# RMSNorm and QKV projection: the last two 128-column stores issued from two queues

## Chip, cores, metric

One core of one Trainium2 chip runs the kernel. The metric is the device time in microseconds (us). Executions of one program scatter by some tenths of a microsecond, so each figure is a median with its range.

## The reference

`x` is 8 x 1024 x 768 in float32, `w_qkv` is 768 x 2304, `gamma` has 768 ones.

```python
rms = np.sqrt(np.mean(x ** 2, axis=-1, keepdims=True) + eps)
x_norm = x / rms * gamma
return np.matmul(x_norm, w_qkv).astype(np.float32)
```

## The kernel before

The 8192 rows are 64 row tiles of 128. For each, SP (the sync engine, which here only issues DMAs) loads `x`, VectorE casts it to bf16, a DMA transpose on SP's queue turns it (`xbar`; `xT<-xb` in the profile), PE (the matmul engine) multiplies it with the resident weights in column blocks of 512, VectorE and ScalarE take turns to bring the blocks out of PSUM (times 1/rms; one such step is an eviction), and SP stores them. In the lines of the profile DVE is VectorE, ACT is ScalarE, PEld are PE's weight loads, and SPq and ACTq are the sequencers of SP and ScalarE, which issue DMAs; L255 is line 255 of the kernel. The author sets the order by writing a planned time beside each piece of work; the plan is sorted and emitted, and every engine then runs its own list in order. So a planned time is only a place in a list: nothing waits for it. The cut below leaves out what `...` stands for, and its comments are mine.

```python
    def width(t, n0):
        return P if t == MT - 1 and n0 >= N - 2 * P else min(NT, N - n0)
    ...
    def store(t, h, n0, nl):
        p0 = PARTS[h][0]
        nc.sync.dma_start(out=of[t * P:(t + 1) * P, n0:n0 + nl], in_=OUT[t, h][:, n0 - p0:n0 - p0 + nl])
    ...
    def evac_at(time, t, n0, eng, gap):
        at(time, evac, t, n0, eng)
        ...
        if t >= MT - 2:
            at(time + gap - 0.5, store, t, h, n0, nl)      # the last two row tiles: a store per block
        elif left[t, h] == 0:
            at(time + gap, store, t, h, *PARTS[h])
    ...
    for t in range(HEAD, MT):                              # HEAD = 6
        ahead = 6.0 if t < HEAD + 5 else 0.0
        ...                                                # load at now - 15 - ahead, cast at now - 8.5 - ahead
        at(now - 7.5 - ahead, xbar, t)
        ...
        for n0 in [*range(0, N, NT)] + [N - P] * (t == MT - 1):
            at(now, mm, t, n0, range(KO))
            now += width(t, n0) * US
            flip ^= 1
            evac_at(now + 0.2, t, n0, "DVE" if flip else "ACT", gap=1.2)
```

The very last 256 columns are computed as two blocks of 128, the first brought out by ScalarE, the second by VectorE. `ahead` gives 6 us of extra lead to the row tiles 6 to 10.

Of the kernel before, what the change touches and what calls it, by code (L numbers as in the profile page):

```python
# [92 lines left out]
def kernel(  # L93
# [8 lines left out]
    nc = tc.nc  # L102
# [6 lines left out]
    of = out.flatten_outer_dims()  # L109
    M, K = xf.shape  # L110
    Kw, N = w_qkv.shape
    assert K == Kw
    P = 128
    KO = K // P
    MT = M // P
# [35 lines left out]
    X, XB, XT, RS, OUT, WF, PM, PT = {}, {}, {}, {}, {}, {}, {}, {}  # L151
# [100 lines left out]

    def store(t, h, n0, nl):
        p0 = PARTS[h][0]
        nc.sync.dma_start(out=of[t * P:(t + 1) * P, n0:n0 + nl], in_=OUT[t, h][:, n0 - p0:n0 - p0 + nl])  # L255



# [12 lines left out]
    def evac_at(time, t, n0, eng, gap):  # L271
        at(time, evac, t, n0, eng)
        h = part(n0)
        nl = width(t, n0)
        left[t, h] = left.get((t, h), PARTS[h][1]) - nl
        if t >= MT - 2:
            at(time + gap - 0.5, store, t, h, n0, nl)
        elif left[t, h] == 0:
            at(time + gap, store, t, h, *PARTS[h])
# [79 lines left out]
```

## Time and profile before

| | before |
|---|---|
| median of the 3 executions known at the prediction | 388.34 us (388.09 to 388.74) |
| span of the profiled execution | 386.86 us |
| PE busy | 379.9 us (98%) |
| last 512-column eviction of VectorE begins | 382.56 us |
| from there to the end of the span, the "tail" | 4.30 us |

The profile is of one execution. The span runs from its first to its last instruction and is some 1.8 us shorter than the device time (388.64 us for this execution). The DMA strips show the mean busy share of the 16 DMA engines in 40 slices of a window, in tenths. The lines themselves are in the prediction.

### The profile page before, as it was taken

What the parts mean: (1) busy time and instruction counts of PE and PEld (TensorE: products, weight loads), DVE (VectorE), ACT (ScalarE), POOL (GpSimd) and SP (SyncE); (2) the same over time, 40 slices, a digit from 0 to 9 for tenths busy, and PEclk for the clock granted to TensorE, in tenths of its full rate; (3) what the DMA queues carried; (4) which work ended last, traced back from release to release, by engine and by line L of the source; (5) the groups of instructions that cost most, each with busy time, mean ns of one, the idle gap of its engine ahead of it and who ended that gap; (6) DMA issues with size and microseconds to landing.
All of it is one profiled execution on the core that took longest, in us unless ns stands there. A gap on an engine that the chain in (4) does not pass through costs nothing.

```text
span 386.9 us, 5470 instructions
## 1 busy us (share of the span) xinstructions
PE 379.9 (98%) x1927; PEld 192.2 (50%) x1965; DVE 153.4 (40%) x307; ACT 181.6 (47%) x365; POOL 6.5 (2%) x14
## 2 busy tenths in 40 slices
PE   8999999999999999999999999999999999999996
PEld 4444655454554554554554554554554554554553
DVE  2744534434333344333344333343333343333332
ACT  4752644453544443544444444544444534434532
POOL 0130000000000000000000000000000000000000
PEclk9999999999999999999999999999999999999999
DMA  8999999999999999999999999999999999999985
GB/s 291 390 281 402 398 318 363 344 338 283 351 297 308 303 295 321 293 300 322 305 289 313 285 318 312 293 309 275 326 311 297 304 317 305 304 306 289 292 264 186
DMA packets 89719, 119.91 MB, mean 310 GB/s; under 512 B 52438, under 2 KB 61532, under 8 KB 89692
## 3 DMA queue, kind: packets, MB, share of 16 engines
q1 hardware_dynamic: 89680, 119.56, 101.2%
q8 instruction: 15, 0.25, 0.3%
q14 instruction: 12, 0.10, 0.1%
q10 hardware_dynamic: 12, 0.00, 0.0%
HBM read 32.25 MB, written 75.50 MB: 279 GB/s over the span
## 4 chain that ended last, share of the span: by engine, by line
PE 89%; DMA 8%; issue 1%; DVE 1%; ACT 1%; SPq 0%
PE pm L235 89%; DMA x_t<-in_x_dram 3%; DMA w_f<-in_w_qkv_dram 2%; DMA xT<-xb 2%; DMA out_dram<-ot 1%; ACT ot L251 1%; DVE ot L249 0%; DVE xb L174 0%; SPq L160 0%; SPq L155 0%; SPq L255 0%; ACT w_b L168 0%
## 5 line engine op out<-in xcount | busy, mean ns | idle before, releaser
L235 PE MATMUL pm<-w_b,xT 128*128 128x512 bf16 (+1 forms) x1888 | 372.1, 357 | 2.1
L235 PEld LDWEIGHTS <-xT 128*128 128x128 bf16 x1926 | 187.9, 98 | 185.5 <-DMA xT<-xb 0.5
L249 DVE TENSOR_SCALAR ot<-pm,rstd 128x512 f32<-128x512 f32 (+1 forms) x161 | 111.5, 695 | 206.1 <-PE pm L235 201.7
L251 ACT ACTIVATE ot<-pm,rstd 128x512 f32<-128x512 f32 (+2 forms) x160 | 102.7, 643 | 191.7 <-PE pm L235 151.0
L185 ACT ACTIVATE sq<-x_t 128x768 bf16<-128x768 f32 x64 | 53.4, 834 | 3.0 <-DMA x_t<-in_x_dram 3.0
L174 DVE CAST xb<-x_t 128x768 bf16<-128x768 f32 x61 | 33.2, 545 | 13.6 <-DMA x_t<-in_x_dram 13.5
L187 ACT ACTIVATE rms<-ssq,eps_sb 128x1 f32<-128x1 f32 x64 | 18.8, 294 | 2.1
L185 ACT ACTIVATION_READ_ACCUMULATOR sq<-x_t 128x1 f32 x64 | 12.2, 191 | 0.0
L166 DVE TENSOR_SCALAR w_b<-w_f,g_sb 128x512 bf16<-128x512 f32 (+1 forms) x16 | 7.7, 499 | 5.9 <-DMA w_f<-in_w_qkv_dram 5.9
L192 DVE RECIPROCAL rstd<-rms 128x1 f32<-128x1 f32 x64 | 9.8, 153 | 0.0
L170 POOL TENSOR_SCALAR w_b<-w_f,g_sb 128x512 bf16<-128x512 f32 (+1 forms) x8 | 5.8, 735 | 23.5 <-DMA w_f<-in_w_qkv_dram 23.5
L284 PE MATMUL pm<-const-bfloat16-1.0 128*128 128x512 bf16 (+1 forms) x14 | 5.4, 539 | 0.8 <-PEq L340 0.8
L168 ACT ACTIVATE w_b<-w_f,g_sb 128x512 bf16<-128x512 f32 (+1 forms) x6 | 3.6, 612 | 2.7 <-DMA w_f<-in_w_qkv_dram 2.7
L212 PE MATMUL pm<-ident_f,x_t 128*128 128x128 f32 x18 | 2.8, 300 | 0.3 <-DMA x_t<-in_x_dram 0.3
L212 PEld LDWEIGHTS pm<-ident_f,x_t 128*128 128x128 f32 x18 | 2.4, 160 | 1.3 <-DMA x_t<-in_x_dram 0.9
L284 PEld LDWEIGHTS <-const-bfloat16-1.0 128*128 128x128 bf16 x14 | 1.5, 126 | 2.7 <-issue 2.7
L176 ACT CAST xT<-pm 128x256 bf16<-128x256 f32 (+1 forms) x5 | 2.3, 458 | 0.9 <-PE pm L212 0.7
L142 ACT ACT_TABLE_LOAD x1 | 1.3, 1283 | 1.4 <-PEq L340 1.4
L174 DVE CAST xT<-pm 128x512 bf16<-128x512 f32 x1 | 0.7, 691 | 1.4 <-PE pm L212 1.4
L267 DVE COPY g_sb<-pm 128x6 f32<-128x6 f32 x1 | 0.2, 164 | 1.9 <-PE pm L266 1.9
L266 PEld LDWEIGHTS pm<-ident_f,g 6*128 6x128 f32 x1 | 0.2, 177 | 1.0 <-issue 1.0
L174 DVE COPY xT<-pm 128x768 bf16<-128x768 bf16 x1 | 0.6, 557 | 0.0
(12 smaller groups left out, 2.5 us busy)
## 6 DMA issues: line engine op xcount, KB each, us to landing
out_dram<-ot SPq DMA_DIRECT2D x124, 512.0 KB, 3.9
x_t<-in_x_dram SPq DMA_DIRECT2D x64, 384.0 KB, 4.2
out_dram<-ot SPq DMA_DIRECT2D x63, 128.0 KB, 3.2
w_f<-in_w_qkv_dram SPq DMA_DIRECT2D x10, 512.0 KB, 7.4
out_dram<-ot SPq DMA_DIRECT2D x8, 256.0 KB, 2.0
w_f<-in_w_qkv_dram SPq DMA_DIRECT2D x4, 256.0 KB, 6.6
xT<-xb SPq DMA_TRANSPOSE x60, 4.3
w_f<-in_w_qkv_dram SPq DMA_DIRECT2D x2, 384.0 KB, 6.1
```

Source lines behind the costliest of these rows:

```text
L166: nc.vector.tensor_scalar(out=o, in0=i, scalar1=g, scalar2=None, op0=mult)
L168: nc.scalar.activation(out=o, in_=i, func=AF.Copy, scale=g, bias=0.0)
L170: nc.gpsimd.tensor_scalar(out=o, in0=i, scalar1=g, scalar2=1.0, op0=mult, op1=mult)
L174: nc.vector.tensor_copy(out=out, in_=in_)
L185: nc.scalar.activation(out=sq, in_=X[t], func=AF.Square, accum_out=ssq)
L187: nc.scalar.activation(out=rms, in_=ssq, func=AF.Sqrt, scale=inv_k, bias=eps_sb)
L192: nc.vector.reciprocal(out=r, in_=RS[t])
L212: nc.tensor.transpose(out=PT[t, h][:, ko - k0, :], in_=X[t][:, ko * P:(ko + 1) * P], identity=ident_f)
L235: nc.tensor.matmul(out=PM[t, n0][:, :nl], lhsT=XT[t][:, ko, :], rhs=w_b[:, ko, n0:n0 + nl], start=(b == 1), stop=(b == KO))
L249: nc.vector.tensor_scalar(out=o, in0=pm[:, :nl], scalar1=RS[t], scalar2=None, op0=mult)
L251: nc.scalar.activation(out=o, in_=pm[:, :nl], func=AF.Copy, scale=RS[t], bias=0.0)
L284: nc.tensor.matmul(out=wps[:, :nl], lhsT=ones[:, :P], rhs=ones[:, :nl], start=True, stop=True)
```

## The change

The last two stores of 128 columns each become ready almost together, but leave from one queue, one after the other. The change issues the first of them from ScalarE, which has just produced it, so that it goes out beside SP's.

```diff
     def store(t, h, n0, nl):
         p0 = PARTS[h][0]
-        nc.sync.dma_start(out=of[t * P:(t + 1) * P, n0:n0 + nl], in_=OUT[t, h][:, n0 - p0:n0 - p0 + nl])
+
+        queue = nc.scalar if t == MT - 1 and n0 == N - 2 * P else nc.sync
+        queue.dma_start(out=of[t * P:(t + 1) * P, n0:n0 + nl], in_=OUT[t, h][:, n0 - p0:n0 - p0 + nl])
```

## The prediction

> **What bounds the kernel now.** I read the page's head first, then the page's chain of waits, then the end of the span with three views: the timeline, the rows of the storing line in short windows, and the DMA strips of short windows. From the page:
>
> ```profile
> span 386.9 us, 5470 instructions
> PE 379.9 (98%) x1927; PEld 192.2 (50%) x1965; DVE 153.4 (40%) x307; ACT 181.6 (47%) x365; POOL 6.5 (2%) x14
> PE 89%; DMA 8%; issue 1%; DVE 1%; ACT 1%; SPq 0%
> ```
>
> PE is busy for 379.9 of 386.9 us and carries 89% of the chain. It is the bound, and the change doesn't touch it. So the change can only act on what follows PE's last matmul. That matmul ends at about 383.2 us (the timeline has the last run of matmuls at 382.81 for 0.39), so the whole tail is 386.86 - 383.2 = 3.66 us, 0.94% of the span. A gain over 2% can't come from there: even a tail of length zero would not give it.
>
> The tail, from the timeline of the last microseconds and from windows of it that hold one or two issues of the storing line each:
>
> ```profile
> 382.56 1.02 DVE L249 TENSOR_SCALAR ot<-pm,rstd 128x512 f32<-128x512 f32 x2 [1.84 <-DMA out_dram<-ot]
> 382.90 0.37 ACT L251 ACTIVATE ot<-pm,rstd 128x128 f32<-128x128 f32 x1 [0.94 <-PE pm L235]
> 383.34 1.30 SPq L255 DMA_DIRECT2D out_dram<-ot  x3
> ...
> 383.23 0.35 DVE L249 TENSOR_SCALAR ot<-pm,rstd 128x128 f32<-128x128 f32 x1
> ...
> L255 SPq DMA_DIRECT2D out_dram<-ot x1: 333/333/333, 383.3 to 383.3; - x1
> ...
> L255 SPq DMA_DIRECT2D out_dram<-ot x2: 383/392/401, 383.8 to 384.2; - x2
> DMA to landing us min/median/max: 1.6/1.6/1.6
> ```
>
> The reader is to see that three evictions become ready almost together: ScalarE's 128 columns at 382.90 + 0.37 = 383.27, VectorE's 512 columns at about 383.31 (0.75 after 382.56), VectorE's 128 columns at 383.58. Their three stores, however, queue behind each other on SP: 256 KB issued from 383.34, the first 64 KB from 383.77, the second 64 KB from 384.24 to 384.64. The last data was ready at 383.58 and its store began to be issued 0.66 us later. That is the delay the change is aimed at. The last store lands 1.6 us after its issue began, 384.24 + 1.6 = 385.8, which agrees with SP's wait at the end:
>
> ```profile
> SPq L354 <- DMA out_dram<-ot: 1.1, 1, 1.1
> ```
>
> After 385.8 there is only the end of the program, semaphores and drains up to 386.86, about 1.08 us that no store shortens.
>
> The decisive view is the DMA strip, first of 384.1 to 385.6 (slots of 37.5 ns), then of 384.2 to 384.7 (12.5 ns):
>
> ```profile
> DMA  0094979798895979599696889884769896631000
> DMA packets 432, 0.39 MB, mean 262 GB/s; under 512 B 48, under 2 KB 304, under 8 KB 432
> q1 hardware_dynamic: 432, 0.39, 76.5%
> ...
> q1 hardware_dynamic: 92, 0.19, 100.2%
> ```
>
> The 16 DMA engines are at work without a hole from 384.17 to about 385.5. All three stores are in there: 432 packets are 128 of 2 KB (the 256 KB), 256 of 512 B (the two of 64 KB) and 48 of under 512 B (16 per store). So the last two stores do not stand alone on an idle DMA; they queue behind the 256 KB store in the engines too.
>
> **What the Trainium skill says.**
> - "DMA: Bandwidth & Descriptors", section "Issuing engines are not separate DMA queues": DMAs from all issuing engines run on the same 16 DMA engines, and issuing from several "will only save the time on the sequencer". The trace can't show it yet for two stores, since only one small load uses ScalarE's queue (the queue with 12 packets, of gamma).
> - Same page, "Queues, rings and completion order": each DMA engine takes turns between the rings that have work, packet by packet. If so, the moved store is interleaved with the 256 KB one rather than run beside it. No view of before shows it.
> - Same page, "Latency and other measured facts": about 0.6 us to the first byte for such queues. Here it is 0.83 us: the strip begins at 384.17 for the issue that began at 383.34; counted from the issue's end it is 0.50.
> - Same page, "Anatomy of one DMA", has a fixed cost of about 2 us (for another path), mostly the receipt of the write. Here the last packets end at 385.5 and SP is released at 385.8, so the receipt takes about 0.3 us; that part stays.
>
> **The change part by part.** It removes one issue from SP (383 ns plus the some 0.05 to 0.1 us that lie between issues on SP) and adds one on ScalarE, directly behind its own eviction. The order of instructions of both kernels shows nothing else moved: same matmuls, same evictions, same stores; only semaphore numbers of the last stores shift by one. The three stores, step by step:
>
> 1. 256 KB store on SP: its data is ready at 383.31, issue 383.34, first byte 384.17. Unchanged.
> 2. First 64 KB on ScalarE's queue: eviction ends 383.27, issue from about 383.30. The only issue there in this trace, gamma's, took 584 ns against 432 to 455 on SP at the same time, and its first packets came 0.97 us after the issue began (0.73 to 1.70, read packet by packet). So first byte at 383.30 + 0.83 to 0.97 = 384.13 to 384.27, against about 384.85 before.
> 3. Second 64 KB on SP: issue right after the first, at about 383.77 in place of 384.24. This is 0.47 us gained on the issue, and by the issue alone the last landing would come at 383.77 + 1.6 = 385.37 in place of 385.84.
> 4. The DMA engines, though, have the same work: 76.5% of 1.5 us is 1.15 us per engine. Check from packets: in the window where only 2 KB packets run, 92 packets in 0.5 us x 16 engines are 87 ns each; from the two windows where 512 B ones run (98 packets at 76.8% of 0.2 us, 78 at 56.0% of 0.2 us, 10 and 16 of them tiny) I get 27 ns for one of 512 B and 7 for a tiny one. Per engine 8 x 87 + 16 x 27 + 3 x 7 = 1.15 us. Begun at 384.17 it can't end before 385.32; now it ends at 385.50. But the engines don't all start together: the completion packets of the 256 KB store come over a spread of 0.17 us (384.85 to 385.02). The engine that starts last, at about 384.34, ends at 384.34 + 1.15 = 385.49 whatever the order of its packets. Before, it ended at 385.51. There is the floor.
>
> So of 0.47 us gained on the issue, 0.02 to at most 0.18 us reach the end, because the DMA engines' own queue was nearly as long as the issue's. I take 0.05 us. Nothing else lies on the path: 388.34 - 0.05 = 388.29, written 388.3.
>
> **The rivals.**
> - *The issue is the bound.* Then the whole 0.47 us comes out: 387.87. For it: both 64 KB stores land 1.6 us after their own issue, and the second one's packets can't start before 384.24 + 0.83 = 385.07. Against it: packets run without a hole through 385.07, so at most a few hundredths of it are waited for. It needs the packets of two queues on one DMA engine to overlap better than those of one. 15%.
> - *The two issues hinder each other.* Two queues issued at the same moment may share what makes the descriptors. At the start, where ScalarE and SP issue together, SP's issues took 0.43 to 0.46 us, though later ones do as well; a lone store here takes 0.33. If the 256 KB issue grows by 0.1 us, everything behind it starts later by that: +0.05 to +0.15 us, 388.4 to 388.5. Interleaving of 512 B packets with 2 KB ones could add some as well. 25%.
> - *The end of the program waits for ScalarE.* Its drain at the end now comes after an issue of 0.4 to 0.6 us, at about 383.9 in place of 383.3. SP waits for data until 385.8 anyway, so this is hidden: 0. Only a landing on ScalarE's queue that is much slower than 1.6 us would show, since the end waits for it as well. It would have to take over 2.5 us from 383.30. Unlikely.
>
> **Range and chances.** All the paths lie within -0.5 and +0.2 us, 0.13% of the time at most. What decides the reading is the spread between executions: 388.09 to 388.74 over three, 0.65 us. Around 388.3 I take half a microsecond to each side: 387.8 to 388.8. Over 2% would be 7.8 us, more than twice the whole tail, so faster and slower get half a per cent each, for a surprise that isn't in this analysis.
>
> **What the profile after would show.** Right: SP's last issue begins at about PE's end + 0.6 in place of + 1.0; one issue on ScalarE right behind its 128-column eviction; about 144 packets more on the queue that had 12; the strip still solid from the first byte to about 1.3 us later; span 386.8 +- 0.1. Step 4 is wrong if the packets end 0.3 us or more earlier after the first byte, or if the strip has holes. Step 1 is wrong if the 256 KB issue takes over 0.4 us. The whole is wrong if the stream of matmuls before 383 us moves by more than a few tenths, which the change gives no reason for.

## The result

Ratios here are the mean time of one kernel's fast runs over the mean of the other's fast runs of the same rounds, so they aren't quite the ratio of the medians.

| | median | range | executions |
|---|---|---|---|
| before | 388.27 us | 388.09 to 388.74 | 6 |
| changed | 389.05 us | 388.30 to 390.63 | 6 |

The ratio is 1.0024 (95% interval 1.0002 to 1.0047). Against the prediction's 388.3 the median is 0.75 us too high and lies above the range, 387.8 to 388.8. The single executions in order are 388.78, 389.32, 388.30, 390.12, 388.47 and 390.63: not a shift, but a scatter of 2.3 us.

**The tail after.** The timeline of the changed kernel's last microseconds (start, duration, engine, what):

```profile
382.67 1.02 DVE L249 TENSOR_SCALAR ot<-pm,rstd 128x512 f32<-128x512 f32 x2 [1.84 <-PE pm L235]
383.01 0.37 ACT L251 ACTIVATE ot<-pm,rstd 128x128 f32<-128x128 f32 x1 [0.94 <-PE pm L235]
383.40 0.40 ACTq L257 DMA_DIRECT2D out_dram<-ot  x1
```

The storing line's issues in the window of 383.3 to 384.2 (on SP two; shortest, median and longest in ns, first and last start):

```profile
L257 SPq DMA_DIRECT2D out_dram<-ot x2: 333/358/382, 383.4 to 383.9; - x2
```

SP's wait for stores at the end (total, times, longest, in us):

```profile
SPq L356 <- DMA out_dram<-ot: 1.7, 1, 1.7
```

The DMA strip of 384.1 to 385.6 and its queues (packets, MB, share of the 16 engines' time):

```profile
DMA  0000188979989989999889989988889799885100
q1 hardware_dynamic: 288, 0.33, 61.8%
q10 hardware_dynamic: 144, 0.07, 14.8%
```

The reader is to see that the change did to the issues what it was meant to: the last store leaves SP at 383.87, 1.20 us after the last 512-column eviction began, where it was 1.68 before. The issue on ScalarE takes 0.40 us, hinders nothing (the 256 KB issue beside it still takes 333 ns), and q10, ScalarE's queue, now carries the 144 packets of the moved store. But the two queues together keep the DMA engines busy for 61.8 + 14.8 = 76.6% of 1.5 us, against 76.5% before. It is the same work, and it ends at almost the same place. SP, done with its issues 0.48 us earlier, waits 1.7 us for the data in place of 1.1.

Counted from the start of the last 512-column eviction, with the packets read one by one in the trace:

| us after the start of that eviction | before | changed |
|---|---|---|
| first packet of the three stores | 1.61 | 1.61 |
| last store issued on SP | 1.68 | 1.20 |
| last packet ends | 2.94 | 2.89 |
| SP released | 3.31 | 3.35 |
| end of the span | 4.29 | 4.33 |

(The views' rounded times give 4.30 for the tail of before.) The gain of 0.48 us at the issue is 0.05 us at the last packet, and then SP is released 0.46 us after it in place of 0.37, so that the end is 0.04 us later. In the tail the change is worth nothing, and it is nowhere near +0.8 us either.

**The body after.** What was not expected is in the first 100 us, where the two programs are the same. PE's weight loads, in a window of 32 to 100 us, wait once in the changed kernel's profile and never in that of before. From the changed kernel's:

```profile
PEld L235 <- DMA xT<-xb: 0.5, 1, 0.5
```

Its chain of waits (start, duration, what) runs through the same spot:

```profile
28.69 38.18 PE pm L235 x203
66.87 6.94 DMA xT<-xb
73.81 0.05 issue
73.86 308.79 PE pm L235 x1584
```

A DMA transpose issued at 66.87 landed 6.94 us later, and PE, which needed it at about 73.3, stood still for 0.5 us. By the plan this is row tile 11, the first without the extra lead: its matmuls begin at 44.0 + 5 x 5.83 = 73.1 us of planned time and its transpose is planned 7.5 us before. In the profile of before, the same transpose, issued at 67.23, landed after 5.8 us, some 0.6 us before PE came to it. So after the first 32 us, in which PE waits for first loads and transposes in both kernels, there is one place where PE's time differs between the two profiles. Two theories came of this:

- *body*: the changed kernel's slow executions are executions in which tile 11's transpose came late, and have nothing to do with the change;
- *queue*: the use of ScalarE's queue costs such executions in some way that the profile of a good one doesn't show.

For the tail, *floor* (the DMA engines are busy anyway; step 4 of the prediction) stands against *landing* (two queues land later, whatever their size) and *issue* (the issue is the bound).

### The profile page after: what moved, and what is told of

Read it like the earlier page. It is cut to its first block, busy times and chain, and to the rows that moved or that the text cites. A ratio compares the mean times of both kernels' runs of the same rounds, so it can differ in the third digit from the quotient of the medians.

```text
span 387.0 us, 5508 instructions
## 1 busy us (share of the span) xinstructions
PE 381.5 (99%) x1965; PEld 191.5 (49%) x1965; DVE 153.2 (40%) x307; ACT 181.6 (47%) x365; POOL 6.5 (2%) x14
## 4 chain that ended last, share of the span: by engine, by line
PE 90%; DMA 8%; DVE 0%; issue 0%; SPq 0%; ACT 0%
PE pm L235 90%; DMA xT<-xb 3%; DMA x_t<-in_x_dram 3%; DMA w_f<-in_w_qkv_dram 2%; DVE ot L249 0%; ACT ot L251 0%; DVE xb L174 0%; SPq L160 0%; SPq L155 0%; ACT w_b L168 0%
## 5 line engine op out<-in xcount | busy, mean ns | idle before, releaser
L235 PE MATMUL pm<-w_b,xT 128*128 128x512 bf16 (+2 forms) x1926 | 374.3, 357 | 0.3 <-DMA xT<-xb 0.2
```

Source lines behind the costliest of these rows:

```text
L235: nc.tensor.matmul(out=PM[t, n0][:, :nl], lhsT=XT[t][:, ko, :], rhs=w_b[:, ko, n0:n0 + nl], start=(b == 1), stop=(b == KO))
```

## The experiments

Unless told otherwise each is timed in 5 rounds against the kernel before, on a chip shared by the kernels of one call (chips 2, 4, 15 and 7; the record of the first result names no chip). "Tail" is always from the start of VectorE's last 512-column eviction to the end of the span.

### The two kernels again: b1, a1, a2, a3, a4, b2

No edit. Expected:

> The kernel before, unchanged, run as if it were a change: how much two sets of executions of one program differ. If the +0.24% of the changed kernel is chance (theory 'body': a few executions lose 1 to 2 us in waits for loads and transposes in the first 80 us, whichever kernel runs), this set too should now and then hold an execution above 389.5 us, and its ratio to before may be off by 0.1 to 0.2%. If the scatter belongs to the change (theory 'queue': the use of ScalarE's queue costs it), this set stays within 388.0 to 388.8 with a ratio of 1.000 +- 0.0007. Tail in the profile, from the start of the last 512-column eviction of VectorE to the end of the span: 386.86 - 382.56 = 4.30 us as before, to within 0.05.

> The changed kernel, unchanged, a second time. Theory 'body' (chance): median 388.2 to 388.5, ratio 1.000 to 1.001, no more executions over 389.5 than the kernel before has. Theory 'queue': again a median near 389 and single executions of 390 and more, ratio 1.002 or above. Theory 'tail' (stores of two queues land later, always): a constant shift of 0.0 to +0.2 us with no scatter, ratio 1.000 to 1.0005. The tail, from the last 512-column eviction's start to the end, was 387.0 - 382.67 = 4.33 us; 4.25 to 4.40 again.

> The changed kernel, unchanged, a third time. Theory 'body': a ratio within 0.9985 and 1.002, either sign, decided by how often tile 11's transpose was late; tail 4.33 us. If it is again at 1.002 or above with executions of 390, while the kernel before has none, then two of three sets show it and chance is no good explanation.

> The changed kernel, unchanged, a fourth time, if chance has it on a third chip. Theory 'body' as before: ratio 0.9985 to 1.002. Open is where the 390.1 and 390.6 us of the first set came from: no execution of any kernel since was above 389.6. If such a one turns up here in the profile, PE's waits before 100 us should hold the difference, and the tail should still be 4.33.

> The changed kernel, unchanged, a fifth time. Theory 'body': ratio 0.9985 to 1.002 and a median of 388.2 to 388.9. If the three executions of 389.3 to 390.6 in its first set were the chip's or the hour's, they should turn up about as often in b2_before_third, or not at all. If they are the changed kernel's own, they should turn up here and not there.

> The kernel before, unchanged, beside a4_after_fifth on the same chip: together with the runs of before that all four share, 14 executions. Ratio 0.999 to 1.001; largest execution 389.0 to 389.5.

| run | kernel | chip | median (range) | ratio to before | 95% interval | tail |
|---|---|---|---|---|---|---|
| b1 | before | 2 | 388.44 (388.22 to 388.82) | 0.9996 | 0.9982 to 1.0010 | 4.31 |
| a1 | changed | 2 | 388.30 (388.17 to 389.12) | 0.9993 | 0.9980 to 1.0005 | 4.33 |
| a2 | changed | 4 | 388.38 (388.25 to 388.90) | 0.9999 | 0.9986 to 1.0011 | 4.32 |
| a3 | changed | 15 | 388.87 (388.21 to 389.14) | 1.0006 | 0.9994 to 1.0019 | 4.33 |
| a4 | changed | 7 | 388.49 (388.21 to 388.85) | 1.0002 | 0.9990 to 1.0014 | 4.33 |
| b2 | before | 7 | 388.30 (388.04 to 388.91) | 0.9998 | 0.9986 to 1.0010 | 4.30 |

Four sets of the changed kernel on four chips have ratios of 0.9993 to 1.0006, whose mean is 1.0000. In 20 executions none is above 389.14, while the kernel before has 389.27 among its executions on chip 2. The +0.24% doesn't come back. The expectation for b1, that such a set now and then holds an execution above 389.5, was not met: no later set of an unmodified kernel had one; nor was that of b2, a largest execution of 389.0 to 389.5 (it was 388.91). The tails repeat to 0.02 us, so a tail can be read from one profile where a time can't.

a1's profile happened to be of its slowest execution, 389.12 us. The timeline of PE's weight loads between 60 and 90 us, first before, then a1:

```profile
59.93 30.14 PEld L235 LDWEIGHTS <-xT 128*128 128x128 bf16 x155
```

```profile
60.10 13.07 PEld L235 LDWEIGHTS <-xT 128*128 128x128 bf16 x69
74.19 15.88 PEld L235 LDWEIGHTS <-xT 128*128 128x128 bf16 x81 [1.02 <-DMA xT<-xb]
```

One unbroken row before, one hole of 1.02 us in a1: its transpose, issued at 66.4, took 7.8 us to land. Nothing else in a1 after 32 us waits for a transpose, and its tail is 4.33.

### More lead for tiles 11 to 13: f1, f2, f3

```diff
-        ahead = 6.0 if t < HEAD + 5 else 0.0
+        ahead = 6.0 if t < HEAD + 8 else 0.0
```

f1 is the kernel before with this edit, f2 and f3 are the changed kernel with it.

> The kernel before, with the row tiles 11 to 13 given the same 6 us of extra lead (load, cast, transpose) that tiles 6 to 10 have. In the profiles so far the transpose of tile 11, issued at about 67 us, landed after 5.8 to 7.8 us, and PE waited for it 0, 0.5, 0, 1.0, 0 and 0.5 us in six profiles. Theory 'body' (that one transpose, late by chance, makes the scatter): no wait of PE for a transpose after 32 us in the profile, all executions within about 0.5 us of each other, and a ratio of 0.998 to 0.9995. Rival 'elsewhere' (the scatter comes from something between executions, or from the first loads): same ratio and scatter as the kernel before.

> The changed kernel with the same extra lead. Theory 'body': times within 0.2 us of f1_lead_before, no execution above 389.0, so that the changed kernel's +0.24% of the first set goes away with a wait 310 us before the changed stores. Theory 'queue' (use of ScalarE's queue costs it): still single executions at 390, and f1 has none. Tail 4.33 us as in both profiles of the changed kernel.

> The changed kernel with the extra lead for tiles 11 to 13 (as f2_lead_after), again. Theory 'body': the spread of its executions stays within 0.5 us on this chip too (0.17 us in f2, 0.35 in f1, 0.29 in g1_best), whatever a4_after_fifth does. If it holds single executions over 389.2, something other than tile 11's transpose makes them.

| run | base | chip | median | range | spread | ratio to before |
|---|---|---|---|---|---|---|
| f1 | before | 4 | 388.29 | 388.12 to 388.47 | 0.35 | 0.9995 |
| f2 | changed | 4 | 388.50 | 388.42 to 388.59 | 0.17 | 1.0000 |
| f3 | changed | 7 | 388.29 | 388.22 to 388.34 | 0.12 | 0.9997 |

The spread is the answer. Without the lead, sets of five have spreads of 0.60 to 0.95 us (b1, b2, a1 to a4). With it, three sets have 0.12 to 0.35, with either tail, and no execution above 388.6. These are sets of five, and one set without the lead, s1 below, had only 0.37. In all three profiles PE's weight loads wait for nothing after 32 us; f2's from 60 to 90 us are one unbroken row:

```profile
60.01 29.92 PEld L235 LDWEIGHTS <-xT 128*128 128x128 bf16 x154
```

That the use of ScalarE's queue makes slow executions is not what f2 and f3 show. But a1 to a4 had no execution of 390 without the lead either, so f2 and f3 tell of the usual scatter and not of where the 390s of the first set came from. The median of f2 lies 0.21 us above that of f1 on the same chip, of which the tails explain 0.05; f3 on another chip doesn't repeat it, and I leave it open.

### Tile 11's transpose made late: w1, w2

The transpose alone is moved down SP's list, in the kernel before: by one store in w1, by two stores and a load in w2.

```diff
-        at(now - 7.5 - ahead, xbar, t)
+        at(now - 7.5 - ahead + 2.5 * (t == HEAD + 5), xbar, t)      # w1;  w2: 4.5
```

> The kernel before, with the transpose of tile 11 put one store later on SP's queue: issued some 2.2 us later, at about 69.5. Theory 'body': PE waits for it 2 to 4 us at about 73 us, and the time grows by that to 390 to 392, with a scatter of a microsecond and more, as the slow executions of the changed kernel showed; the tail stays 4.30. Rival 'elsewhere': the wait is hidden or small, the time stays within 0.5 us of the kernel before.

> The kernel before, with the transpose of tile 11 put two stores and a load later on SP's queue (w1: one store later, PE's wait 1.2 us, time +0.7 to +0.9). Theory 'body': PE waits some 3 us for it at about 73 us and the time is 390 to 392, so that one late transpose is enough to give an execution as slow as the slowest of the first set. Rival: the transpose lands faster when issued later, the wait stays under 2 us and the time under 389.8; then 390.6 needs more than this wait.

Measured: w1 389.31 us (388.86 to 389.62), ratio 1.0018 (1.0005 to 1.0032). Here I had expected too much: the transpose left at 68.3, only 1.1 us later than before, landed after 6.0, and PE waited 1.2 us. w2 gave 391.10 us (390.36 to 392.27, 6 executions), ratio 1.0073 (1.0058 to 1.0089), with a wait of 2.3 us where some 3 were expected. PE's weight loads in w2, from 60 to 90 us:

```profile
60.09 13.28 PEld L235 LDWEIGHTS <-xT 128*128 128x128 bf16 x70
75.64 14.38 PEld L235 LDWEIGHTS <-xT 128*128 128x128 bf16 x74 [2.27 <-DMA xT<-xb]
```

The hole is 2.27 us in the execution that took 390.57. The spread over w2's executions is 1.9 us, but only this one was profiled, and the two slowest, 392.19 and 392.27, have a granted clock of 0.995 and 0.996 where every other execution here has 0.998 to 1.000; so how much of the spread is this wait is not shown. The profiled executions of all kernels with full stores and without extra lead, sorted by that one wait (o1 and s1 are told of below):

| PE's wait near 73 us | device time of that execution |
|---|---|
| none (before, b1, s1, a2, a3, b2) | 388.16 to 388.64 |
| 0.5 to 0.6 (changed, o1, a4) | 388.73 to 388.85 |
| 1.0 (a1) | 389.12 |
| 1.2 (w1) | 389.31 |
| 2.3 (w2) | 390.57 |

So one late transpose is enough to make an execution of 390.6, and the time follows it about one for one. The traces also say where the 0.5 us among those without this wait come from. Count the evictions of both engines in order of time. The 31st begins between 45.55 and 46.09 us; from it to the 71st are 46.68 us in every profile where PE doesn't wait near 73 us, and 46.68 plus 0.39 (o1) to 2.16 us (w2) where it does; from the 71st to VectorE's last 512-column eviction are 289.80 us in all 18 profiles, t1 and t2 included. So between profiles of these kernels PE's stream differs in two places only, before 46 us and at tile 11. The slowest without the wait, the kernel before at 388.64, has its 31st eviction at 46.09 us; the fastest, b2 at 388.16, at 45.59.

### Small stores, one after the other and side by side: t1, t2

The last three stores (the last 512 columns and both of 128) write 16 rows in place of 128, so the result is wrong. t1 is the kernel before with this edit, t2 the changed kernel. In the cut `....` stands for `nc.sync` in t1 and `queue` in t2.

```diff
+        rows = 16 if t == MT - 1 and n0 >= N - 6 * P else P
-        ....dma_start(out=of[t * P:(t + 1) * P, n0:n0 + nl], in_=OUT[t, h][:, n0 - p0:n0 - p0 + nl])
+        ....dma_start(out=of[t * P:t * P + rows, n0:n0 + nl], in_=OUT[t, h][:rows, n0 - p0:n0 - p0 + nl])
```

> The kernel before, but its last three stores move 16 rows in place of 128, one eighth of the bytes (so the result is wrong on purpose: 112 rows of 768 columns aren't written). The DMA engines' own queue is then about 0.2 us, and only the issues are left. The last store is issued 1.68 us after the last 512-column eviction's start, as before; its first byte comes 0.83 later, at 2.51, the end of data at about 2.6, the tail is some 3.9 to 4.0 us.

> The changed kernel with the same 16-row stores (wrong on purpose in the same way). If step 3 of the prediction holds (0.47 us of issue gained) and step 4 is why it didn't show (the DMA engines were busy anyway), the data now end at about 2.15 us and the tail is 0.35 to 0.45 us shorter than that of t1_small_sequential. If two queues simply don't overlap in issuing, or a store over two queues lands later whatever its size, the tail differs by less than 0.1 us.

The timeline of the issues and the DMA strip of 383.5 to 385.5 (slots of 50 ns), first t1, then t2:

```profile
382.51 1.02 DVE L249 TENSOR_SCALAR ot<-pm,rstd 128x512 f32<-128x512 f32 x2 [1.84 <-DMA out_dram<-ot]
383.29 1.27 SPq L256 DMA_DIRECT2D out_dram<-ot  x3
...
DMA  1000000000007382122000131000000221000000
```

```profile
382.24 1.02 DVE L249 TENSOR_SCALAR ot<-pm,rstd 128x512 f32<-128x512 f32 x2 [1.84 <-DMA out_dram<-ot]
382.97 0.39 ACTq L258 DMA_DIRECT2D out_dram<-ot  x1
383.02 0.82 SPq L258 DMA_DIRECT2D out_dram<-ot  x2
...
DMA  0000000394743220122100000000000000000000
```

In t1 three bursts stand apart, one per issue, with nothing between them; in t2 there are two close together. Counted from the eviction, the last packet ends at 2.72 us in t1 and at 2.27 in t2; the tails are 4.07 and 3.63. t1's tail was expected at 3.9 to 4.0 us, a little too short, and the difference at 0.35 to 0.45. With small stores the very same change is worth 0.44 us, close to the whole of the 0.46 us that it saves in issuing here (the last issue begins at 1.22 us in place of 1.68). That settles the tail: *floor* is right, since the issue's gain comes out once the engines have less to move; *landing* is wrong, since from last packet to SP's release both take 0.37 to 0.38 us; and *issue* is wrong for the real sizes. In both, the DMA engines have 0.2 us of work each; in the kernels proper 1.15. Which DMA engine ends last, and so the inner working of step 4, isn't shown: the trace doesn't name the engine of a packet.

### The other store over ScalarE's queue: s1

```diff
-        queue = nc.scalar if t == MT - 1 and n0 == N - 2 * P else nc.sync
+        queue = nc.scalar if t == MT - 1 and n0 == N - P else nc.sync
```

> The last 64 KB store (VectorE's columns) goes over ScalarE's queue, the first stays on SP. Theory 'queue': the same use of the queue, so the same scatter, ratio 1.002. Theory 'body': ratio 1.000 +- 0.001. Theory 'tail': the issue on SP of the first small store is at +0.43 us behind the 256 KB one as before, that of the second starts once VectorE's eviction ends; the data of the three stores is the same 1.15 us per DMA engine, so the tail is 4.30 +- 0.1 us as in both kernels.

Measured: 388.23 us (388.03 to 388.40), ratio 0.9987 (0.9975 to 1.0000), tail 4.25 us. It uses ScalarE's queue as much as the changed kernel and is the quietest of the sets without extra lead (spread 0.37 us), which speaks against *queue* once more. Its last packet ends at 2.90 us, as in the changed kernel; SP is released 0.37 us later, not 0.46. That step takes 0.45 to 0.46 us in all seven profiles with the changed stores (the first one, a1 to a4, f2, f3) and 0.36 to 0.38 in the eight of full stores with SP's queue alone (before, b1, b2, f1, w1, w2, o1, g1) and here. What the 0.09 us are stays open.

### One store in place of two: o1, and with the lead: g1

```diff
-        if t >= MT - 2:
+        if t == MT - 1 and n0 >= N - 2 * P:
+            if n0 == N - P:
+                at(time + gap - 0.5, store, t, h, N - 2 * P, 2 * P)
+        elif t >= MT - 2:
             at(time + gap - 0.5, store, t, h, n0, nl)
```

> The two stores of 128 columns are made one of 256 columns, issued on SP once both evictions are done: 128 packets of 1 KB in place of 256 of 512 B. No use of ScalarE's queue, so theory 'queue' expects no scatter: 388.0 to 388.7. If the DMA engines' own queue is what sets the tail (my step 4), the data get shorter by 8 x (2 x 27 - about 47) ns = 0.06 us per engine and one issue goes, so the tail is 4.1 to 4.3 us: no longer than before though the last-but-one data waits 0.3 us for the last. If the issue were the bound, the single issue at 383.77 would land at about 385.4, a tail of 3.85 us.

> One store of 256 columns at the end (as o1) and the extra lead of f1 together. By the profiles o1's tail is 4.09 us against 4.30, f1 takes away the wait for tile 11's transpose: 388.3 - 0.2 = 388.1, all executions within 0.5 us, ratio 0.9985 to 0.9995. If the tail's 0.2 us don't reach the time of the whole, 388.3 as f1.

o1's DMA strip from 384.1 to 386.1 (50 ns slots):

```profile
DMA  0000000759989699898978999999741000000000
DMA packets 288, 0.39 MB, mean 197 GB/s; under 512 B 32, under 2 KB 160, under 8 KB 288
```

The same 0.39 MB are 288 packets in place of 432: 128 of 1 KB, 45 ns each, where 256 of 512 B took 27 each. The engines have 1.07 us of work in place of 1.15, the last packet ends 2.81 us after the eviction in place of 2.94, and the tail is 4.09 us in place of 4.29. Some 0.13 us of that are the shorter work and the missing third store; 0.07 us lie behind SP's release, in the end of the program (0.91 us in place of 0.98), and I can't say why. The time doesn't show it: 388.42 us (388.06 to 389.42), ratio 0.9996 (0.9983 to 1.0009), because the scatter between executions is larger; o1's profiled execution had a wait of 0.5 us for tile 11's transpose.

g1 has both edits, one store and the lead, in the kernel before: 388.00 us (387.92 to 388.21), ratio 0.9988 (0.9975 to 1.0002) to a kernel before at 388.46 (388.21 to 388.94) on the same chip; tail 4.11. It is the fastest version here in its median. The gain is 0.1%, and its interval still includes 1, so it isn't clear of the noise.

## Why the prediction was wrong, and where it was right

Where it was wrong:

- **The range.** The step that failed is "What decides the reading is the spread between executions: 388.09 to 388.74 over three, 0.65 us. Around 388.3 I take half a microsecond to each side." Three executions don't show how far a distribution reaches that hangs on one late transpose. Of the first six of the changed kernel three were above 389; of 20 later ones two were, at 389.12 and 389.14. So the median of that one set fell outside; the medians of the four later sets are 388.30 to 388.87 and centre on 388.4. The centre was right to 0.1 us and the width was not: with two executions of 390 in six, one side should have been a microsecond or more wide.
- **The path.** "Nothing else lies on the path" failed as well: PE's wait for tile 11's transpose lies on it, with 0.5 us in the changed kernel's profile and 2.3 in w2's. The prediction said that the whole is wrong "if the stream of matmuls before 383 us moves by more than a few tenths, which the change gives no reason for". The stream does move, in either kernel, by up to a microsecond in the profiles (the last 512-column eviction begins between 382.03 and 383.01 us in the kernels with neither w1's nor w2's edit). The change indeed gives no reason. What could have warned me was in the profile of before: a DMA row at 9, that is 90% or more, nearly all through, and, where transposes land after a median of 4.3 us, one that took 5.8 with some 6.4 to be had (67.23 to about 73.65, by when PE asked for it in the changed kernel's profile, whose stream ran 0.30 us earlier).
- **Small readings.** "Both 64 KB stores land 1.6 us after their own issue" isn't in the view: it holds one landing, that of the second store. From the last packet to SP's release it is 0.37 us, not about 0.3, and from there to the end 0.98, not about 1.08. The span after was put at 386.8 +- 0.1 and was 387.0, mostly through the body (0.11 us). None of these decides the range.

Where it was right:

- **PE is the bound, and the tail is all that the change touches.** The tail is 0.04 us longer, and in the profiles the rest of the difference lies before it; no profile of the changed kernel speaks against this.
- **Steps 1 to 3, the issues.** 0.47 us gained was predicted, 0.48 measured; the 256 KB issue unchanged at 333 ns; ScalarE's issue 0.40 us. Its first packet came 1.04 us after the issue began, a little later than the 0.83 to 0.97 predicted.
- **Step 4, the floor.** A gain of 0.02 to 0.18 us was predicted to reach the end. 0.05 reached the last packet, as predicted; t1 and t2 show the reason by taking it away. Beyond the last packet the prediction expected no difference, and there are 0.09 us, which turned a gain of 0.05 into a loss of 0.04. That is below what the times here can show.
- **The rivals.** *The issue is the bound* (15%) is refuted by the two tails (0.48 us earlier at the issue, 0.04 later at the end), and t1 and t2 show why. *The two issues hinder each other* (25%): the durations of the issues in the tail refute that they do. Its last sentence, that interleaved packets could add some, isn't refuted: the 0.09 us after the last packet, whose cause is open, could be of this kind. *The end waits for ScalarE* didn't happen: its landing, 2.4 us after issue, comes 0.2 us before SP's last.
- **The class.** Within 2% was given 99%, and it is.

What stays open: none of the three slow executions of the changed kernel's first set was profiled, and its chip isn't on record. That tile 11's transpose made them is the likely cause: it makes executions of that size (w2), it scatters by itself (5.8 to 7.8 us to landing), the usual scatter shrinks when it is given time (f1 to f3), and the granted clocks of the three (0.999 to 1.000) are those of ordinary executions. But that it did so in those three is inferred, not shown, and why so often in that set isn't explained. Two of its six executions are above 390, while of the 74 other executions of the two unmodified kernels, the six of before in its own comparison included, none is above 389.27. The longest such wait in a profile of an unmodified kernel is 1.0 us. Something of that chip or hour is a rival that no run here settles.

## What to carry to other kernels

Here, issuing stores from two queues shortened the tail when the DMA engines had nothing to do in the time gained (0.44 us with small stores), and not when they were busy (0.04 us longer with full ones). So look at the DMA strip between the first and last packet before counting an issue's time as a gain. Fewer, larger packets took 0.2 us off the tail here (o1), though not visibly off the time. Before trusting a difference of a few tenths of a per cent, look for the one wait that decides by chance, here a transpose planned with 7.5 us of lead on DMA engines that were nearly full, and give it slack; here the spread of a set of five fell from 0.60 to 0.95 us to 0.12 to 0.35. Read a small local effect from the profile by counting from an event just before it, which here repeated to 0.02 us while whole times scattered by 0.9.

## What the Trainium skill lacked or had wrong

- "DMA: Bandwidth & Descriptors", section "Issuing engines are not separate DMA queues": the runs agree that the engines are the same: the two queues together kept them as busy as the one, 76.6% against 76.5% of 1.5 us. It calls the sequencer's time "usually small relative to the DMA itself". With stores of 16 rows the saved issue time was worth 0.44 us of tail, against 0.2 us of work per DMA engine, though a store then still took 1.4 to 1.6 us from issue to landing.
- Same page, "Queues, rings and completion order": taking turns between queues fits what the packets show, though the trace doesn't name the engine of a packet, so the turns themselves aren't seen. In the changed kernel ScalarE's 512 B packets begin from 1.77 to 2.66 us, among SP's 2 KB ones from 1.61 to 2.53, and that store of 64 KB landed 2.4 us after its issue.
- Same page, "Latency and other measured facts": about 0.6 us to the first byte, and it lacks from which moment that counts. On SP the stores here show 0.83 us from the start of the issue and 0.50 from its end; on ScalarE 1.04 from the start (0.88 when the stores were small), beside SP's packets.
- Same page, "Anatomy of one DMA": about 2 us of fixed cost, most of it the receipt, given there for the other path. Here the time from the last packet to SP's release is 0.37 us, and 0.46 in the changed kernel.
- Same page, on DMA transposes: nothing on how their time to landing scatters beside other transfers. Here one and the same transpose took 5.8 to 7.8 us to land in the kernels that leave it in its place, against a median of 4.3 over the kernel. No page warns that such a wait can make part of the spread between executions (0.60 to 0.95 us with it in six sets of five, 0.12 to 0.35 in three with more lead).
